# Up products of the feed-forward layers in seven blocks, down sums in three groups: one Trainium2 core

## The chip, the core and the metric

One core of a Trainium2 chip runs the whole program. The metric is device time in microseconds (us), the median of three runs. Each core has five engines with queues of their own: PE (TensorE, matrix products), DVE (VectorE), ACT (ScalarE), POOL (GpSimd) and SP (SyncE, which here only issues DMAs). They wait for one another through semaphores.

## What is computed

Two layers work on 512 tokens of width 1024, each layer a feed-forward (FFN), a mixer (even: gated linear and forgetting attention; odd: sparse attention) and a second FFN; a final norm follows. There are therefore four FFNs, called ffn0 to ffn3 here, with the even mixer between ffn0 and ffn1 and the odd one between ffn2 and ffn3. The change touches the FFNs, with d_ff = 2816:

```python
def swiglu(h, w_in, w_out):
    a, b = jnp.split(h @ w_in, 2, axis=-1)
    return (jax.nn.silu(a) * b) @ w_out

def reference(x, norm_g, ...):
    for layer in range(DEPTH):
        x = x + 0.5 * swiglu(rmsnorm(x, g[0]), ffn_w_in[layer, 0], ffn_w_out[layer, 0])
        x = x + mixer(rmsnorm(x, g[1]), ...)
        x = x + 0.5 * swiglu(rmsnorm(x, g[2]), ffn_w_in[layer, 1], ffn_w_out[layer, 1])
    return rmsnorm(x, final_norm_g)
```

All data are fp32. The kernel multiplies in the type float32r, with every operand split exactly into a high and a low part, so that one block product w x becomes three matmuls: high by high, high by low, low by high (`mm3`).

## The kernel before

The state X lies in SBUF as eight tiles of 128 channels by 512 tokens. **Norm.** The norm's gain is applied to X at once and its 1/rms later: `scaled` makes the parts XGH[i] (ACT, L139) and XGL[i] (DVE, L140) of X_i times the gain; `sumsq` adds X_i squared into one tile, the square on ACT (L152) and the add on POOL (L156). `rstd_cols` reduces that tile with four matmuls (L181) and takes the reciprocal root in short steps on ACT (L168, L169) and DVE (L184, L170 to L173); `rstd_tile` spreads the result over the partitions with four transposes (L195) into R.

**Way up.** `ffn` walks over 22 f tiles of 128 hidden channels. For each, `up_mm` loads 1024 KB of weights, splits them piece by piece (512 columns; high part on ACT L80, low part on DVE L84, pool `wsp` with six buffers) and runs 2 (gate and up) x 8 (channel tiles) x 3 matmuls of 512 tokens into two PSUM banks. `up_act` multiplies both by R on DVE (L231, L235), takes silu on ACT, multiplies (L236) and splits the result h in two (L209, L210). R is needed from `up_act(0)` on, and two or three `up_mm` stand ahead of it. **Way down.** After 12 of the 22 f tiles, `down(0, d)` sums f tiles 0 to 10 for each of eight output tiles d: 704 KB of weights, 11 x 3 matmuls of 512 tokens, and one DVE step (L247) that adds half of the sum to X_d. After the rest, `down(1, d)` does the same for f tiles 11 to 21, and `after(d)` starts the next layer's `scaled` and `sumsq` of X_d.

**Between layers.** The out projection of a mixer (`out_units`, 24 matmuls of 512 tokens for each d) ends with one DVE add (L323) and `after(d)`. Each weight is loaded into the two-buffer pool `wraw`, on SP's queue. **Order.** PE's instructions run in the order in which the code is written; a scheduler orders the other engines' queues, each of which then runs strictly in its order. **Start.** Nine matmuls of ones run ahead of the data; X and the first weights come in small pieces, interleaved, and `up_mm(0)` takes each channel tile as it comes.

In the addresses of the built program, the tiles of XGH and XGL start 32 bytes past a multiple of 64, and h, the mixers' outputs (the operand x of the out projection) and whi start on a multiple.

## Time and profile before

| | |
|---|---|
| median of 3 runs | 2019.51 us |
| the runs | 2015.47 to 2019.82 us |
| span of the profiled execution | 2014.5 us |
| PE busy | 1981.9 us (98%) |
| DVE, ACT, POOL busy | 1012.7, 765.4, 219.8 us |
| mean granted clock of PE | 0.993 |

The span is the time from the first to the last instruction of one profiled execution, whose own time is not given; the runs last 1.0 to 5.3 us longer than the span. The page says how long each engine was busy; the windows say it for one stretch; the timeline gives single instructions with their starts; a matmul's own duration overlaps the next one's, so its cost is the distance from start to start (called its pitch below).

### The profile page before, as it was taken

The page shows a single profiled execution, that of the slowest core. Times are in us where ns is not written, and L with a number is a line of the kernel's source. Part 1 is how long each engine was busy: PE and PEld are TensorE (multiplying, and loading weights), DVE is VectorE, ACT ScalarE, POOL GpSimd, SP SyncE. Part 2 cuts the span into 40 slices and gives each one's busy share as a digit, 9 for nine tenths or more (in the row PEclk, how much of TensorE's full clock was granted, in tenths as well). Part 3 has the DMA queues.
Part 4 walks back from the last instruction along what each step waited for, and adds up shares of the span by engine and source line. Part 5 has one row for each costly group of instructions (what it writes and reads, how often), then busy time and mean ns, then how long its engine had stood idle before and what let it go on. Part 6 is the DMA issues. An engine that isn't in the chain of part 4 may idle for free. (4 is left out here: it accounts for less than half of the span.)

```text
span 2014.5 us, 24213 instructions
## 1 busy us (share of the span) xinstructions
PE 1981.9 (98%) x9298; PEld 1602.2 (80%) x9298; DVE 1012.7 (50%) x1780; ACT 765.4 (38%) x1386; POOL 219.8 (11%) x230
## 2 busy tenths in 40 slices
PE   8999999999999999999999999999999999999997
PEld 6888888887878888888888888887777788888886
DVE  5543444457565444344444434444898654434443
ACT  4432333344454332233433323343537543322332
POOL 2000000100261000000100000001358410000001
PEclk9999999999899999999999999999999999999999
DMA  5223222213333222222222232223357122232222
GB/s 172 84 85 114 84 98 87 102 65 101 105 98 106 84 98 86 99 104 79 100 105 84 88 111 84 92 90 116 93 147 177 55 104 103 74 105 105 84 87 71
DMA packets 44212, 197.75 MB, mean 98 GB/s; under 512 B 6072, under 2 KB 7272, under 8 KB 29888
## 3 DMA queue, kind: packets, MB, share of 16 engines
q1 hardware_dynamic: 41440, 191.65, 28.8%
q10 hardware_dynamic: 2304, 4.20, 0.8%
q8 instruction: 73, 1.20, 0.2%
q0 software_dynamic: 352, 0.36, 0.1%
q14 instruction: 43, 0.35, 0.1%
HBM read 178.03 MB, written 2.15 MB: 89 GB/s over the span
## 5 line engine op out<-in xcount | busy, mean ns | idle before, releaser
L80 ACT ACTIVATE whi<-wraw 128x512 fp32r<-128x512 f32 (+2 forms) x667 | 411.6, 618 | 941.5 <-PE s L126 325.4
L84 DVE TENSOR_TENSOR wlo<-wraw,whi 128x512 fp32r<-128x512 f32 (+2 forms) x643 | 441.7, 688 | 496.1 <-ACT whi L80 462.7
L127 PE MATMUL s<-xgh,wlo 128*128 128x512 f32 x576 | 229.3, 398 | 1.9 <-DVE wlo L84 1.9
L126 PE MATMUL s<-xgl,whi 128*128 128x512 f32 x576 | 229.7, 399 | 1.3 <-DVE xgl L140 1.2
L125 PE MATMUL s<-xgh,whi 128*128 128x512 f32 x576 | 229.5, 398 | 1.1 <-ACT whi L80 1.1
L156 POOL TENSOR_TENSOR ss<-ss,sq 128x512 f32<-128x512 f32 x48 | 64.2, 1338 | 1495.6 <-ACT sq L152 1495.3
L125 PE MATMUL ps<-xgh,whi 128*128 128x512 f32 (+2 forms) x544 | 217.4, 400 | 1.6 <-DVE x L834 1.6
L127 PE MATMUL ps<-xgh,wlo 128*128 128x512 f32 (+2 forms) x544 | 215.6, 396 | 0.0
L126 PE MATMUL ps<-xgl,whi 128*128 128x512 f32 (+2 forms) x544 | 215.4, 396 | 0.0
L125 PE MATMUL pt<-xgh,whi 128*128 128x512 f32 x384 | 152.4, 397 | 0.0
L127 PE MATMUL pt<-xgh,wlo 128*128 128x512 f32 x384 | 152.3, 397 | 0.0
L126 PE MATMUL pt<-xgl,whi 128*128 128x512 f32 x384 | 152.2, 396 | 0.0
L127 PEld LDWEIGHTS s<-xgh,wlo 128*128 128x128 f32 x576 | 108.9, 189 | 29.6 <-DVE wlo L84 3.2
L126 PEld LDWEIGHTS s<-xgl,whi 128*128 128x128 f32 x576 | 108.9, 189 | 29.5 <-DVE xgl L140 3.5
L125 PEld LDWEIGHTS s<-xgh,whi 128*128 128x128 f32 x576 | 109.0, 189 | 28.2 <-ACT whi L80 1.7
L125 PEld LDWEIGHTS ps<-xgh,whi 128*128 128x128 f32 (+2 forms) x544 | 101.5, 187 | 28.0 <-issue 3.5
L127 PEld LDWEIGHTS ps<-xgh,wlo 128*128 128x128 f32 (+2 forms) x544 | 101.5, 187 | 25.8
L126 PEld LDWEIGHTS ps<-xgl,whi 128*128 128x128 f32 (+2 forms) x544 | 101.6, 187 | 24.3
L125 PE MATMUL s<-h,whi 128*128 128x512 f32 x264 | 102.7, 389 | 0.0
L126 PE MATMUL s<-h,whi 128*128 128x512 f32 x264 | 102.7, 389 | 0.0
L127 PE MATMUL s<-h,wlo 128*128 128x512 f32 x264 | 102.7, 389 | 0.0
L209 ACT ACTIVATE h<-tb 128x512 fp32r<-128x512 f32 x88 | 55.5, 632 | 115.9 <-DVE tb L236 115.7
(270 smaller groups left out, 3354.6 us busy)
## 6 DMA issues: line engine op xcount, KB each, us to landing
wraw<-in_ffn_in_dram SPq DMA_DIRECT2D x87, 1024.0 KB, 4.8
wraw<-in_ffn_out_dram SPq DMA_DIRECT2D x64, 704.0 KB, 4.1
x<-x SPq DMA_DIRECT2D x62, 128.0 KB, 2.4
wraw<-in_even_fox_dram SPq DMA_DIRECT2D x4, 1024.0 KB, 4.8
wraw<-in_even_out_dram SPq DMA_DIRECT2D x4, 1024.0 KB, 5.7
wraw<-in_odd_q_dram SPq DMA_DIRECT2D x8, 512.0 KB, 3.5
T<-rvd ACTq DMA_DIRECT2D x16, 256.0 KB, 4.3
wraw<-in_odd_out_dram SPq DMA_DIRECT2D x4, 1024.0 KB, 5.8
```

The source lines that it names most:

```text
L80: nc.scalar.activation(hi, x, AF.Copy)
L84: nc.vector.tensor_sub(lo, x, hi.bitcast(F32))
L125: mm(ps, w[0], x[0], start=first, stop=False)
L126: mm(ps, w[0], x[1], start=False, stop=False)
L127: mm(ps, w[1], x[0], start=False, stop=last)
L156: nc.gpsimd.tensor_tensor(self.ss, self.ss, sq, op=OP.add)
L209: self.nc.scalar.activation(o[0], x, AF.Copy)
```

## The change

Two f tiles make a pair p, 11 pairs for each FFN. The weights of a pair form blocks a11, a21, a12, a22 (of 128 partitions by 1024 columns: two f tiles times four channel tiles; the channel tiles split in even and odd ones, the columns in gate and up). The tokens are cut in two halves of 256 columns. A two by two block product that takes eight block products is written in the Strassen-Winograd form, with seven (p1 to p7) of sums and differences of blocks:

- `side` forms four combinations of weight blocks on DVE for each pair, and `make` splits seven blocks of 1024 columns (ACT L159, DVE L160), up to two products ahead. The pool `wsp` now holds three blocks of 1024 columns.
- `combined` takes the place of `scaled` ahead of an FFN: for each pair of channel tiles it forms seven token operands of 256 columns and splits them into TH and TL (L222, L223), with four differences on DVE (L229, L236 to L238). In the addresses of the built program, all operands of TH and TL start 32 bytes past a multiple of 64.
- `product` runs 2 x 4 x 3 = 24 matmuls of 256 columns for each product, 168 for each pair in place of 96 of 512. PE's order for a pair r is p1(r), p4(r-1), p5, p2, p6, p3, p7.
- The results are put together on ACT (copies c1, c5, c2) and DVE (L357, L363, L370, L374, L375); R multiplies the gate half (L365), and h is split for a pair at once (L378, L379).
- R is made between p6 and p3 of pair 0 of every FFN.
- The way down runs in three groups of pairs (4, 4 and 3) over all eight d. R is applied again to the up half in `down_end`, in two DVE steps (L396, L397).
- The weights of the mixers are split in pieces of up to 1024 columns; the nine matmuls of ones are gone; X and the blocks of pair 0 are loaded alternately; block a22 goes to a pool `wx` that lies where a mixer's memory lay.

```diff
+GROUPS = ((0, 4), (4, 8), (8, 11))
+HT = S // 2
+B11, T1, B21, B22, T2, T4, T3 = range(7)
...
+class Products:
+    ORDER = ("p1", "p5", "p2", "p6", "p3", "p7", "p4")
+    def __init__(self, b, src):
+        self.b, self.src, self.parts, self.blocks = b, src, {}, {}
+    def place(self, p, early):
+        b = self.b
+        w = self.blocks.setdefault(p, {})
+        if early:
+            raw = b.wraw.tile([128, 2048], F32, name="wraw")
+            w["a11"], w["a21"] = raw[:, :1024], raw[:, 1024:]
+            w["a22"] = b.wx.tile([128, 1024], F32, name="a22", bufs=2)
+        else:
+            w["a12"] = b.wx.tile([128, 1024], F32, name="a12", bufs=1)
+    def fetch(self, p, n):
+        c = ("a11", "a21", "a12", "a22").index(n) * 1024
+        self.b.nc.sync.dma_start(self.blocks[p][n], self.src[p, :, c:c + 1024])
+    def load(self, p, early):
+        if p < NP and ("a11" if early else "a12") not in self.blocks.get(p, ()):
+            self.place(p, early)
+            for n in ("a11", "a21", "a22") if early else ("a12",):
+                self.fetch(p, n)
+    def side(self, p, q):
+        w, v = self.blocks[p], self.b.nc.vector
+        if q == "p1":
+            return w["a11"]
+        if q == "p2":
+            return w["a12"]
+        if q == "p4":
+            return w["a22"]
+        if q == "p5":
+            w["s"] = self.b.wx.tile([128, 1024], F32, name="ws", bufs=1)
+            v.tensor_add(w["s"], w["a21"], w["a22"])
+            return w["s"]
+        if q == "p6":
+            v.tensor_sub(w["s"], w["s"], w["a11"])
+            return w["s"]
+        if q == "p3":
+            v.tensor_sub(w["a12"], w["a12"], w["s"])
+            return w["a12"]
+        v.tensor_sub(w["a21"], w["a11"], w["a21"])
+        return w["a21"]
+    def make(self, p, q):
+        if (p, q) in self.parts:
+            return
+        b = self.b
+        x = self.side(p, q)
+        o = b.wtile(1024)
+        b.nc.scalar.activation(o[0], x, AF.Copy)
+        b.nc.vector.tensor_sub(o[1], x, o[0].bitcast(F32))
+        self.parts[p, q] = o
...
-    def load_w(self, src, n, pool_lo=False, piece=512, cuts=()):
+    def load_w(self, src, n, pool_lo=False, piece=1024, cuts=()):
...
+    def combined(self, i, gcol):
+        nc, v = self.nc, self.nc.vector
+        j, x = i // 2, self.X[:, i].rearrange("p (h t) -> p h t", h=2)
+        def parts(n, m, src):
+            h, l = self.TH[j][:, n:n + m], self.TL[j][:, n:n + m]
+            nc.scalar.activation(h, src, AF.Copy)
+            v.tensor_sub(l, src, h.bitcast(F32))
+        if i % 2 == 0:
+            e = self.E = self.xp.tile([128, 3, HT], F32, name="te")
+            nc.scalar.activation(e[:, 0:3:2], x, AF.Copy, scale=gcol)
+            v.tensor_sub(e[:, 1], e[:, 2], e[:, 0])
+            parts(B11, 2, e[:, 0:2])
+        else:
+            e, o = self.E, self.xp.tile([128, 5, HT], F32, name="to")
+            nc.scalar.activation(o[:, 0:2], x, AF.Copy, scale=gcol)
+            parts(B21, 2, o[:, 0:2])
+            v.tensor_sub(o[:, 2], o[:, 1], e[:, 1])
+            v.tensor_sub(o[:, 3], o[:, 0], o[:, 2])
+            v.tensor_sub(o[:, 4], o[:, 1], e[:, 2])
+            parts(T2, 3, o[:, 2:5])
...
-        if first:
-            p = self.bank("o")
-            for _ in range(9):
-                nc.tensor.matmul(p[:, :128], self.ones, self.ones, start=True, stop=True)
...
+        def product(p, q, bank, t, fresh):
+            hi, lo = W.parts[p, q]
+            for f in range(2):
+                o = bank[:, f * HT:f * HT + HT]
+                for j in range(KT // 2):
+                    c = slice((f * 4 + j) * 128, (f * 4 + j) * 128 + 128)
+                    xh, xl = TH[j][:, t], TL[j][:, t]
+                    for i, (w, x) in enumerate(((hi, xh), (hi, xl), (lo, xh))):
+                        mm(o, w[:, c], x, start=fresh and f == j == i == 0, stop=j == 3 and i == 2, skip_group_check=True)
...
+            if q == "p1":
+                d = st[p] = {"a": self.bank("ps")}
+                product(p, q, d["a"], B11, True)
+                d["c1"] = copy("c1", d["a"], 1)
+                return
+            d = st[p]
+            if q == "p5":
+                d["b"] = self.bank("pt")
+                product(p, q, d["b"], T1, True)
+                d["c5"] = copy("c5", d["b"], 1)
+            elif q == "p2":
+                c = self.bank("s")
+                product(p, q, c, B21, True)
+                d["t"] = self.ft.tile([128, 2, 2, HT], F32, name="ta", bufs=2)
+                v.tensor_add(d["t"][:, :, 0], d["c1"], three(c))
+            elif q == "p6":
+                product(p, q, d["a"], T2, False)
+                d["c2"] = copy("c2", d["a"], 1)
+            elif q == "p3":
+                product(p, q, d["b"], B22, False)
+                v.tensor_add(d["t"][:, :, 1], d["c2"], three(d["b"]))
+                t = d["t"].rearrange("p f h t -> p f (h t)")
+                v.tensor_mul(t, t, R()[:, None, :].to_broadcast([128, 2, S]))
+                self.table = "silu"
+                nc.scalar.activation(t, t, AF.Silu)
+            elif q == "p7":
+                product(p, q, d["a"], T3, False)
+                v.tensor_add(d["c5"], d["c5"], three(d["a"]))
+            else:
+                product(p, q, d["a"], T4, False)
+                t = d["t"]
+                v.tensor_mul(t[:, :, 1], t[:, :, 1], d["c5"])
+                v.tensor_mul(t[:, :, 0], t[:, :, 0], three(d["a"]))
+                h = [self.hp.tile([128, 2, S], F32R, name=x) for x in ("hh", "hl")]
+                t = t.rearrange("p f h t -> p f (h t)")
+                nc.scalar.activation(h[0], t, AF.Copy)
+                v.tensor_sub(h[1], t, h[0].bitcast(F32))
+                H[p] = h
+                del st[p]
...
+        def down_end(d, bank, R):
+            t = self.ft.tile([128, S], F32, name="dn", bufs=1)
+            nc.vector.scalar_tensor_tensor(t, bank, 0.5, R, op0=OP.mult, op1=OP.mult)
+            nc.vector.tensor_add(self.X[:, d], self.X[:, d], t)
+        tags = ("s", "s", "s", "pt", "o")
+        Rt = []
+        R = lambda: Rt[0]
+        def round_(p, seq):
+            rc = None
+            for i, (r, q) in enumerate(seq):
+                for x in seq[i:i + 3]:
+                    W.make(*x)
+                if q == "p5" and (r + 1, "p1") in seq:
+                    W.load(r + 1, True)
+                if q == "p7":
+                    W.load(r + 1, False)
+                if (r, q) == (0, "p6"):
+                    rc = self.rstd_cols("o")
+                if (r, q) == (0, "p3"):
+                    Rt.append(self.rstd_tile(rc, "s"))
+                if (r, q) != (NP - 1, "p4"):
+                    run(r, q, R)
+        W.load(0, True)
+        W.load(0, False)
+        for g, (a, b) in enumerate(GROUPS):
+            last = b == NP
+            seq = []
+            for p in range(a + 1 if g else a, min(b + 1, NP)):
+                ps = [(p, q) for q in Products.ORDER[:6]]
+                if p:
+                    ps.insert(1, (p - 1, "p4"))
+                seq += ps
+            round_(a, seq + [(NP - 1, "p4")] * last)
+            banks = {}
+            def begin(d):
+                w = down_w(g, d)
+                w.split(0)
+                banks[d] = w, self.bank(tags[d % 5])
+            def sums(d, pairs):
+                down_mm(g, d, *banks[d], pairs)
+            def end(d):
+                down_end(d, banks.pop(d)[1], R())
+                if last:
+                    after(d)
+            begin(0)
+            begin(1)
+            if last:
+                self.next_in()
+                self.lnexp()
+                sums(0, range(a, b - 1))
+                run(NP - 1, "p4", R)
+                sums(1, range(a, b - 1))
+                for d in range(2):
+                    sums(d, [b - 1])
+                    end(d)
+                begin(2)
+            for d in range(2 if last else 0, KT):
+                if d + 1 < KT and d + 1 not in banks:
+                    begin(d + 1)
+                sums(d, range(a, b))
+                if d == KT - 2:
+                    W.load(b + 1, True)
+                end(d)
...
-        w = self.load_w(src, n, pool_lo, 512 // m * m)
+        w = self.load_w(src, n, pool_lo, 1024 // m * m)
...
         yield "last"
+        self.next_in()
...
-            self.wsp = pool("wsp", 6)
+            self.wsp = pool("wsp", 3)
...
+                for i, n in ((0, 0), (1, "a11"), (2, 0), (3, "a21"), (4, 0), (5, "a22"), (6, 0), (7, "a12")):
```

`self.next_in()` opens the pool of the next layer's operands; `copy` is an ACT copy out of PSUM, L336.

**The start, DVE.** Before, the queue took one operand of 512 tokens at a time between two pieces of weights (`xgl`, `wlo`):

```order
L140 SCALAR_TENSOR_TENSOR xgl0_91<-X_78,gn_79,xgh0_83 128x512
L84 TENSOR_TENSOR wlo_127<-wraw_107,whi_126 128x256
L84 TENSOR_TENSOR wlo_131<-wraw_107,whi_130 128x256
L140 SCALAR_TENSOR_TENSOR xgl1_92<-X_78,gn_79,xgh1_84 128x512
L140 SCALAR_TENSOR_TENSOR xgl2_93<-X_78,gn_79,xgh2_85 128x512
```

Now (te and to are the scratch tiles of `combined`; the rows are those on channel tiles 4 and 5 and the first on 6, the 17th to the 28th of the queue):

```order
L229 TENSOR_TENSOR te_159<-te_159 128x256
L223 TENSOR_TENSOR tl1_99<-to_147,th1_95 128x768
L150 TENSOR_TENSOR wraw_105<-wraw_105 128x1024
L223 TENSOR_TENSOR tl2_100<-te_159,th2_96 128x512
L236 TENSOR_TENSOR to_167<-to_167,te_159 128x256
L238 TENSOR_TENSOR to_167<-to_167,te_159 128x256
L237 TENSOR_TENSOR to_167<-to_167 128x256
L223 TENSOR_TENSOR tl2_100<-to_167,th2_96 128x512
L229 TENSOR_TENSOR te_179<-te_179 128x256
L160 TENSOR_TENSOR wlo_212<-ws_209,whi_211 128x1024
L223 TENSOR_TENSOR tl2_100<-to_167,th2_96 128x768
L223 TENSOR_TENSOR tl3_101<-te_179,th3_97 128x512
```

The operand tl3 that the last quarter of p1 reads now stands behind 26 DVE steps, among them two weight combinations and two splits.

**From the even mixer into ffn1, DVE.** Before, the last adds of the out projection (L323) and the operands of ffn1:

```order
L323 TENSOR_TENSOR X_78<-ps_5095,X_78 128x512
L84 TENSOR_TENSOR wlo_5202<-wraw_5182,whi_5201 128x512
L140 SCALAR_TENSOR_TENSOR xgl6_97<-X_78,gn_79,xgh6_89 128x512
L84 TENSOR_TENSOR wlo_5270<-wraw_5265,whi_5269 128x512
L323 TENSOR_TENSOR X_78<-ps_5138,X_78 128x512
L84 TENSOR_TENSOR wlo_5274<-wraw_5265,whi_5273 128x512
L140 SCALAR_TENSOR_TENSOR xgl7_98<-X_78,gn_79,xgh7_90 128x512
```

Now (L517 is the same add, ws_5955 the block for p5 of pair 0):

```order
L517 TENSOR_TENSOR X_78<-ps_5854,X_78 128x512
L229 TENSOR_TENSOR te_5888<-te_5888 128x256
L223 TENSOR_TENSOR tl3_5692<-te_5888,th3_5688 128x512
L517 TENSOR_TENSOR X_78<-ps_5896,X_78 128x512
L236 TENSOR_TENSOR to_5922<-to_5922,te_5888 128x256
L238 TENSOR_TENSOR to_5922<-to_5922,te_5888 128x256
L237 TENSOR_TENSOR to_5922<-to_5922 128x256
L223 TENSOR_TENSOR tl3_5692<-to_5922,th3_5688 128x512
L142 TENSOR_TENSOR ws_5955<-wraw_5944,a22_5945 128x1024
L223 TENSOR_TENSOR tl3_5692<-to_5922,th3_5688 128x768
L150 TENSOR_TENSOR wraw_5944<-wraw_5944 128x1024
L160 TENSOR_TENSOR wlo_5958<-ws_5955,whi_5957 128x1024
```

The split for p5 stands behind both halves of the work on the last two channel tiles, where the weights of the first f tiles were done ahead of it.

**R in ffn1, DVE.** Before:

```order
L184 TENSOR_SCALAR Ra_5255<-o_5250 128x4
L84 TENSOR_TENSOR wlo_5367<-wraw_5358,whi_5362 128x512
L170 TENSOR_TENSOR Ra_5255<-Ra_5255,rs_y_5258 128x4
L171 TENSOR_TENSOR Ra_5255<-Ra_5255,rs_y_5258 128x4
L172 TENSOR_SCALAR Ra_5255<-Ra_5255 128x4
L173 TENSOR_TENSOR Rc_5257<-rs_y_5258,Ra_5255 128x4
```

Now (wraw_5997 is block a11 of pair 1):

```order
L283 TENSOR_SCALAR Ra_6071<-o_6066 128x4
L150 TENSOR_TENSOR wraw_5997<-wraw_5997 128x1024
L160 TENSOR_TENSOR wlo_6108<-wraw_5997,whi_6107 128x1024
L269 TENSOR_TENSOR Ra_6071<-Ra_6071,rs_y_6074 128x4
L270 TENSOR_TENSOR Ra_6071<-Ra_6071,rs_y_6074 128x4
L271 TENSOR_SCALAR Ra_6071<-Ra_6071 128x4
L272 TENSOR_TENSOR Rc_6073<-rs_y_6074,Ra_6071 128x4
```

The four last steps of R now stand behind a split for p1 of the next pair, whose buffer is the one that p6 reads.

## Rows read from the trace of the kernel before

**Rows 1.** The page: busy time, share of the span and instructions of each engine.

```profile
PE 1981.9 (98%) x9298; PEld 1602.2 (80%) x9298; DVE 1012.7 (50%) x1780; ACT 765.4 (38%) x1386; POOL 219.8 (11%) x230
```

**Rows 2.** Windows: length, busy us (instructions) of each engine, granted clock, DMA.

```profile
20.00:22.00 2.00, 2.00 (x5) 1.62 (x6) 2.00 (x3) 0.64 (x2) 0.95 (x1) 0.50 0.00 0
200.00:330.00 130.00, 130.00 (x559) 104.93 (x558) 58.25 (x89) 43.46 (x68) 0.00 (x0) 1.00 0.26 90
800.00:900.00 100.00, 100.00 (x434) 81.30 (x434) 41.37 (x64) 29.31 (x47) 0.00 (x0) 1.00 0.29 99
940.00:970.00 30.00, 30.00 (x132) 24.56 (x131) 14.58 (x23) 12.42 (x20) 1.30 (x1) 1.00 0.27 91
```

**Rows 3.** Waits of PE: who waited for whom, total, times, longest.

```profile
PE pt L466 <- DVE pts L450: 3.9, 6, 1.0
PE s L426 <- DVE l L430: 3.5, 1, 3.5
```

**Rows 4.** PE's timeline, out projection into ffn1: start, duration, engine, line, operation, operands.

```profile
636.81 0.39 PE L125 MATMUL ps<-x,whi 128*128 128x512 f32 x1
...
642.02 0.39 PE L127 MATMUL ps<-x,wlo 128*128 128x512 f32 x1
642.25 0.40 PE L125 MATMUL s<-xgh,whi 128*128 128x512 f32 x1
...
645.06 0.40 PE L125 MATMUL s<-xgh,whi 128*128 128x512 f32 x1
```

**Rows 5.** PE's timeline in a mixer's products of 256 columns, moving whi.

```profile
404.01 0.28 PE L125 MATMUL ps<-whi,xgh 128*128 128x256 f32 x1
...
405.09 0.28 PE L125 MATMUL ps<-whi,xgh 128*128 128x256 f32 x1
```

**Rows 6.** Groups of instructions by form: count, busy us, mean ns of one, idle before.

```profile
L80 ACT ACTIVATE whi<-wraw 128x512 fp32r<-128x512 f32 x592 | 373.6, 632 | 851.3 <-PE s L126 288.5 <-PE ps L126 244.8 <-PE pt L126 190.9
L80 ACT ACTIVATE whi<-wraw 128x384 fp32r<-128x384 f32 x65 | 34.2, 526 | 86.2 <-PE s L126 36.9 <-PE ps L126 22.5 <-PE pt L126 20.0
L139 ACT ACTIVATE xgh<-X,gn 128x512 fp32r<-128x512 f32 x48 | 34.5, 720 | 17.0 <-DVE X L247 8.2 <-DVE X L323 6.2 <-DMA X<-in_x_dram 2.6
L450 DVE COPY pts<-pt 128x512 f32<-128x512 f32 x24 | 16.4, 681 | 5.8 <-PE pt L445 5.8
L450 DVE COPY pts<-pt 128x256 f32<-128x256 f32 x24 | 10.1, 419 | 0.0
L156 POOL TENSOR_TENSOR ss<-ss,sq 128x512 f32<-128x512 f32 x48 | 64.2, 1338 | 1495.6 <-ACT sq L152 1495.3
```

**Rows 7.** DVE's timeline in the out projection of the even mixer.

```profile
624.76 1.43 DVE L84 TENSOR_TENSOR wlo<-wraw,whi 128x512 fp32r<-128x512 f32 x1 [0.29 <-ACT whi L80]
626.13 0.69 DVE L323 TENSOR_TENSOR X<-ps,X 128x512 f32<-128x512 f32 x1
626.74 0.68 DVE L84 TENSOR_TENSOR wlo<-wraw,whi 128x512 fp32r<-128x512 f32 x1
```

**Rows 8.** POOL's timeline beside it.

```profile
624.35 1.29 POOL L156 TENSOR_TENSOR ss<-ss,sq 128x512 f32<-128x512 f32 x1 [3.78 <-ACT sq L152]
```

**Rows 9.** DVE's timeline at the start.

```profile
5.18 0.75 DVE L140 SCALAR_TENSOR_TENSOR xgl<-X,gn,xgh 128x512 fp32r<-128x512 f32 x1 [4.18 <-ACT xgh L139]
...
11.05 1.85 DVE L84 TENSOR_TENSOR wlo<-wraw,whi 128x256 fp32r<-128x256 f32 x2
...
15.20 2.92 DVE L84 TENSOR_TENSOR wlo<-wraw,whi 128x256 fp32r<-128x256 f32 x2
```

**Rows 10.** PE's timeline at the start; the second row is the 49th matmul of data.

```profile
5.50 0.79 PE L125 MATMUL s<-xgh,whi 128*128 128x512 f32 x1 [0.24 <-ACT whi L80]
...
25.46 0.40 PE L125 MATMUL pt<-xgh,whi 128*128 128x512 f32 x1
```

**Rows 11.** DVE's timeline, R in ffn1.

```profile
655.15 0.16 DVE L170 TENSOR_TENSOR Ra<-Ra,rs_y 128x4 f32<-128x4 f32 x1
...
655.74 0.16 DVE L173 TENSOR_TENSOR Rc<-rs_y,Ra 128x4 f32<-128x4 f32 x1
```

**Rows 12.** DMA issues: queue, count, size, median us from issue to landing.

```profile
wraw<-in_odd_q_dram SPq DMA_DIRECT2D x8, 512.0 KB, 3.5
wraw<-in_odd_uv_dram SPq DMA_DIRECT2D x2, 512.0 KB, 4.3
```

174 lines of the change are left out of this document (82 added, 92 removed).

## The prediction

> **What bounds the kernel now.** I read the busy shares first [rows 1]: PE works 1981.9 of 2014.5 us, DVE half of the time, ACT less. The windows say the same for each stretch of an FFN [rows 2]: between 200 and 330 us and between 800 and 900 us PE is busy without a break at full clock, DVE 41 to 45% and ACT 29 to 33%; and the change-over from ffn1 to ffn2 (940 to 970) has no gap either. The waits of PE are small, and the two largest lie in the attention [rows 3]. So the time of an FFN is its count of matmuls times their pitch, and whatever takes columns from PE counts in full as long as the other engines keep up. The reader should hold on to two things: the price of one matmul by its size, and how much DVE has left.
>
> **The price of a matmul.** In the out projection, where the moving operand starts on a multiple of 64 bytes, 23 matmuls of 512 columns take 642.02 - 636.81 = 5.21 us, 227 ns each. Right behind, with XGH and XGL, 12 take 2.81 us, 234 ns each [rows 4]. Matmuls of 256 columns with moving whi take 1.08 us for nine, 120 ns [rows 5]. The 227 and the 120 differ by the 107 ns of 256 columns, so each matmul has a fixed part of 13 ns whatever its length; the 7 ns on XGH and XGL I put down to their start address, since it is what sets them apart in the program. TH and TL start in the same way, and no row shows 256 columns with such a moving operand. Its bounds are 120 ns (no extra) and 127 ns (the 7 ns once for each matmul); between lies 120 x 234 / 227 = 124 ns (an extra for each column). Since the fixed part has proved to go by matmul, I take 127.
>
> By the Trainium skill (TensorE: Matmul & The Clock Gate, Back-to-back issue gap) an isolated matmul of N columns takes N / 2.4 + 2.5 ns on a warm engine, with no word on a start address. That would be 216 ns and 109 ns; the rows disagree with both, by 11 ns. By the page's figures a pair would gain 96 x 0.216 - 168 x 0.109 = 2.4 us, close to what the rows give without an extra.
>
> **What the seven products give.** A pair was 96 x 0.234 = 22.46 us and becomes 168 x 0.127 = 21.34 us: 1.12 us, over 44 pairs 50 us. At 124 ns it is 20.8 us and 72 us in all; at 120 ns 20.2 us and 101 us. The way down keeps its 528 matmuls of 512 columns in each FFN.
>
> **Does DVE keep up in steady state?** A pair costs DVE seven splits, four combinations, the product by R and the split of h, 13 steps of 1024 columns, and five of 512. From 256 to 512 columns a DVE step grows from 419 to 681 ns [rows 6], so 1024 columns take 0.68 + 2 x 0.26 = 1.2 us; queued steps start 0.08 us earlier than they end (0.61 apart, 0.69 long [rows 7]), so 1.13 us in a row. 13 x 1.13 + 5 x 0.61 = 17.7 us against 21.3 us of PE. ACT's step of 1024 columns takes 0.632 + 4 x 0.106 = 1.06 us [rows 6], and its 7 splits, 3 copies and the work on h stay under 13 us. PE remains the bound, with a DVE that goes from 45% to above 80%. The three buffers in `wsp` cover 3 us each, more than one split of 1.06 + 1.2 us. I put steady state at no stall; what is lost is lost at the seams, where the cover is thin.
>
> **The seams, one by one.**
>
> *R in each FFN.* PE needs R's column form for the transposes ahead of p3. In the DVE queue its last two to four steps now stand behind a split for the next pair's p1, and that split waits for p6's end, because p6 reads its buffer. After p6, PE therefore waits for ACT's high part (1.06), DVE's low part (1.2) and up to four steps at 0.2 us [rows 11]: 3.0 us, four times 12. Before, these steps followed one split of a free buffer, with the next `up_mm` running on PE. Bounds: 8 (2 us each, if ACT's part is half hidden) and 17 (with part of p3 at half clock after the wait, as in 20 to 22 us [rows 2]).
>
> *The start.* The last quarter of p1 needs tl3's first operand. Up to and with it stand 27 DVE steps: 13 of 256 columns (0.34), seven of 512 (0.61), three of 768 (0.87), four of 1024 (1.13), in all 15.8 us. The first can begin at 5.2 us, where the first XGL was made [rows 9]: 21.0 us. POOL's adds of squares run beside them; in rows 9 two short DVE steps took 1.85 and 2.92 us instead of 0.8, so 1.1 us more for each add that is met. With seven adds at 0.9 us the operand is there at 27 us. PE then has 15 matmuls of p1, p5 and p2 left, 63 x 0.127 = 8 us, and stands at 35 us with 9.1 us of work done: 26 us behind an ideal start. Before, 48 matmuls (11.2 us) were done at 25.46 us [rows 10]: 14.2 behind. The loss is 12; with a clock that is down after the waits [rows 2] I take 13. Bounds: 6 (POOL costs nothing) and 18. The nine matmuls of ones are part of this.
>
> By the Trainium skill (SBUF — State Buffer, SBUF: two separate sides) a DVE step with two SBUF inputs and a POOL step that reads SBUF exclude one another for the whole step. The trace agrees: a DVE split queued at 624.76 took 1.43 us and ended 0.55 us after POOL's add of 1.29 us had [rows 7, 8]. At the full 1.34 us for each of seven adds [rows 6] the start would lose 3 us more; that lies within the bound.
>
> *From a mixer into ffn1 and ffn3.* After the last matmul of the out projection the queue still holds, in series: for channel tile 6 the scale on ACT (0.72), a difference (0.42), both parts (0.63 and 0.68), 2.5 us; for tile 7 the add (0.69), scale (0.72), three differences (1.0) and a split (0.6), 3.0 us; the combination for p5 (1.13), a split of 768, a combination and p5's own split (0.87 + 1.13 + 1.13). That is 9.8 us, and 11.8 with two POOL adds. PE can do p1 and two more matmuls meanwhile, 26 x 0.127 = 3.3 us. Before, `up_mm(0)` covered 11 us of such work, and its weights had been split earlier. Stall 6.5 to 8.5; I take 8, twice 16, bounds 10 and 22. Block a22's transfer waits for the same last matmul, because its memory is the mixer's, and lands 3.5 to 4.3 us later [rows 12]; that is hidden behind tile 7, but is next in line.
>
> *From ffn1 to ffn2.* For two output tiles d DVE does four steps of `down_end` (2.4), the operands of an even and an odd channel tile (0.95 + 2.5) and two weight splits of 768 (1.7): 7.6 us, for eight 30.5. With five steps of 1024 for pair 0 (5.7) and seven POOL adds (6) it is 42 us. PE's cover is 8 x 18 x 0.227 = 32.7 and 1.1 of p1. I take 8; bounds 2 and 14.
>
> *The rest.* The last p4 of an FFN leaves a chain of 0.69 + 1.06 + 1.2 = 2.95 us under 12 matmuls (2.7 us), the short groups of 18 matmuls (4.1 us) leave little for `down_end` and `scaled`, and the mixers' first pieces are twice as long: 5 in all, bounds 0 and 10.
>
> Sum of losses: 12 + 13 + 16 + 8 + 5 = 54 us; the ends add up to 26 and 81, and since they are five separate things I expect 42 to 66.
>
> **The sum.** The profiled span of 2014.5 - 50 + 54 = 2018.5; the median of the runs lies 5.0 us above the span, so 2023.5, rounded to **2024 us**, with 2012 to 2036 for this case. Runs of this kernel can tell 0.2%, 4 us, from no change.
>
> **Rivals.**
>
> *TH and TL cost no extra (faster).* At 120 ns the gain is 101 and the time 2019.5 - 101 + 54 = 1972. For it speaks that no row shows the extra at this size; against it that it is steady on XGH and XGL. Break-even with before lies where the gain equals 54: 20.46 us saved down to 21.23 for a pair, 126.4 ns for a matmul. At 124 ns the time is 2019.5 - 72 + 54 = 2002.
>
> *The seams are half as dear (faster).* If the scheduler's queue lets DVE work ahead in the gaps that I filled, 27 instead of 54: 1997. Against it: each queue runs strictly in order.
>
> *DVE becomes the bound (slower).* It decides from the point where a pair on DVE exceeds 21.3 us, 3.6 us above the 17.7. Each product's split needs ACT's part first and a buffer that PE frees two products later, so waits add to the busy time. At 22 us a pair the stalls would add 44 x 0.7 = 31: 2055. Against it: 16% of slack, and buffers a product ahead.
>
> **How the numbers follow.** Forecast 0.55 (of it 0.1 under 2015.5, 0.13 within 4 us of before, the rest above); no extra 0.18; an extra by column 0.07; cheap seams 0.1; DVE bound 0.1. Faster: 0.1 + 0.18 + 0.06 + 0.09 = 0.43. Within 0.2%: 0.13 + 0.02 = 0.15. Slower: 0.32 + 0.1 = 0.42. Both signs hold much, so the range reaches from 1970, the case without an extra, to 2044, part of the way to a DVE bound.
>
> **What would show it.** The pitch of matmuls on TH and TL in the timeline (127, 124 or 120 ns) decides the first term; a pair in steady state should take 21.3 us with PE busy throughout and DVE 80 to 90%. Waits of PE for L272 should total 10 to 13 us, at the start p1 should wait for L223 until about 27 us, and p5 of ffn1 and ffn3 should wait for L159 and L160 by some 8 us. It is wrong if PE waits for DVE in every pair, or if the seams show half of these waits.

## The result and the profile after

The changed kernel takes **1968.1 us** (median, 1967.1 to 1969.3), against 2019.7 for the kernel before in the same series: ratio 0.974 with a 95% interval of 0.9725 to 0.9757. I had forecast 2024 us with a range from 1970 to 2044. The direction was wrong, and the time lies just below the range, at the rival in which TH and TL cost no extra (1972 us). Two errors of opposite sign made that: the gain from the matmuls was 127 us and not 50, and the seams lost 78 us and not 54.

The page of the kernel after; busy time, share of the span and instructions of each engine, beside [rows 1]:

```profile
span 1965.6 us, 30669 instructions
PE 1872.4 (95%) x12448; PEld 1682.0 (86%) x12448; DVE 1481.5 (75%) x1929; ACT 908.5 (46%) x1275; POOL 226.8 (12%) x218
```

PE has 110 us less to do, and 49 us of it show in the span: PE is idle for 93 us where it was idle for 33. DVE works half as much again. The windows (length, busy us and instructions of PE, weight loads, DVE, ACT, POOL, then PE's granted clock) show where; the first is a steady stretch of ffn0, the others are the seams into ffn1, ffn2 and ffn3, and answer to [rows 2]:

```profile
60.00:120.00 60.00, 60.00 (x517) 60.00 (x516) 56.85 (x56) 33.74 (x37) 0.00 (x0) 1.00 0.30 97
...
640.00:660.00 20.00, 12.31 (x80) 11.90 (x80) 17.33 (x17) 8.82 (x13) 0.99 (x1) 0.83 0.28 93
...
996.00:1016.00 20.00, 14.91 (x105) 14.42 (x105) 17.31 (x23) 9.18 (x15) 2.49 (x2) 0.82 0.23 80
1600.00:1620.00 20.00, 14.25 (x93) 13.71 (x91) 17.36 (x19) 8.76 (x11) 1.27 (x1) 0.74 0.26 94
```

In steady state PE has no gap although DVE is 95% busy there: PE remains the bound, by little. At the seams PE works 62 to 75% of the time, and at a lower clock. Who waited for whom (total, times, longest), for [rows 3]:

```profile
PE ps L332 <- ACT th L222: 15.2, 3, 7.5
PE ps L332 <- ACT whi L159: 12.8, 1, 12.8
PE s L294 <- DVE Rc L272: 11.4, 4, 3.0
PE pt L332 <- ACT whi L159: 9.0, 2, 4.5
PE ps L332 <- DVE tl L223: 7.8, 5, 3.5
```

These are the seams of the prediction: operands of the token side (L222, L223) at the start and into ffn2, R (L272) once in each FFN, p5's weights (L159) into ffn1 and ffn3. The price of a matmul is read from PE's timeline (start, duration):

```profile
249.84 0.28 PE L332 MATMUL ps<-th,wlo 128*128 128x256 f32 x1
...
251.94 0.28 PE L332 MATMUL ps<-th,wlo 128*128 128x256 f32 x1
```

18 matmuls in 2.10 us are 117 ns each, 10 less than I took and 3 less than the lower bound that [rows 5] gave.

### The profile page after: what moved, and what is told of

It is laid out like the page before. It is cut to its first block, busy times and chain, and to the rows that moved or that the text cites. A ratio compares the mean times of both kernels' runs of the same rounds, so it can differ in the third digit from the quotient of the medians.

```text
span 1965.6 us, 30669 instructions
## 1 busy us (share of the span) xinstructions
PE 1872.4 (95%) x12448; PEld 1682.0 (86%) x12448; DVE 1481.5 (75%) x1929; ACT 908.5 (46%) x1275; POOL 226.8 (12%) x218
## 4 chain that ended last, share of the span: by engine, by line
PE 82%; DVE 12%; ACT 2%; issue 2%; DMA 1%; SPq 0%; POOL 0%; DVEq 0%; ACTq 0%; POOLq 0%
PE ps L332 25%; PE pt L332 13%; PE s L332 6%; PE s L199 6%; PE s L200 6%; PE s L198 6%; PE ps L198 3%; PE ps L199 3%; PE ps L200 3%; DVE tl L223 2%; DVE acc L1108 1%; PE s L621 1%; PE pt L198 1%; PE pt L199 1%; PE pt L200 1%
## 5 line engine op out<-in xcount | busy, mean ns | idle before, releaser
L332 PE MATMUL ps<-th,whi 128*128 128x256 f32 x1408 | 395.5, 281 | 28.0 <-ACT th L222 15.2
L332 PE MATMUL ps<-tl,whi 128*128 128x256 f32 x1408 | 395.2, 281 | 7.8 <-DVE tl L223 7.8
L332 PE MATMUL ps<-th,wlo 128*128 128x256 f32 x1408 | 394.6, 280 | 1.0 <-DVE wlo L160 1.0
L332 PEld LDWEIGHTS ps<-th,whi 128*128 128x128 f32 x1408 | 266.4, 189 | 29.3 <-ACT th L222 15.9
L332 PEld LDWEIGHTS ps<-tl,whi 128*128 128x128 f32 x1408 | 266.4, 189 | 9.7 <-DVE tl L223 9.1
L332 PEld LDWEIGHTS ps<-th,wlo 128*128 128x128 f32 x1408 | 266.5, 189 | 1.3 <-DVE wlo L160 1.3
L159 ACT ACTIVATE whi<-a 128x1024 fp32r<-128x1024 f32 x132 | 140.2, 1062 | 154.1 <-PE pt L332 50.4
L332 PE MATMUL pt<-th,whi 128*128 128x256 f32 x704 | 200.9, 285 | 9.0 <-ACT whi L159 9.0
L199 PE MATMUL s<-hl,whi 128*128 128x512 f32 x528 | 206.0, 390 | 0.9 <-DVE hl L379 0.9
L198 PE MATMUL s<-hh,whi 128*128 128x512 f32 x528 | 205.6, 389 | 0.0
L200 PE MATMUL s<-hh,wlo 128*128 128x512 f32 x528 | 205.5, 389 | 0.0
L160 DVE TENSOR_TENSOR wlo<-a,whi 128x1024 fp32r<-128x1024 f32 x132 | 160.9, 1219 | 7.9 <-ACT whi L159 7.9
L159 ACT ACTIVATE whi<-wraw 128x1024 fp32r<-128x1024 f32 x88 | 93.4, 1061 | 145.6 <-PE ps L332 55.8
L396 DVE SCALAR_TENSOR_TENSOR dn<-s,R 128x512 f32<-128x512 f32 x72 | 49.7, 690 | 131.4 <-PE s L200 131.3
```

The lines of the kernel that those rows point to most:

```text
L159: b.nc.scalar.activation(o[0], x, AF.Copy)
L160: b.nc.vector.tensor_sub(o[1], x, o[0].bitcast(F32))
L198: mm(ps, w[0], x[0], start=first, stop=False)
L199: mm(ps, w[0], x[1], start=False, stop=False)
L200: mm(ps, w[1], x[0], start=False, stop=last)
L332: mm(o, w[:, c], x, start=fresh and f == j == i == 0, stop=j == 3 and i == 2, skip_group_check=True)
```

## The experiments

| run | what it changes | median us | ratio to before (95%) |
|---|---|---|---|
| after | | 1968.1 | 0.9741 (0.9725 to 0.9757) |
| e1_align | after, TH, TL, XGH, XGL on multiples of 64 | 1987.1 | 0.9854 (0.9826 to 0.9881) |
| e2_before_align | before, XGH, XGL on multiples of 64 | 2013.9 | 0.9973 (0.9963 to 0.9983) |
| e3_r_late | after, R behind p3 | 1952.5 | 0.9673 (0.9653 to 0.9692) |
| e4_p2_in_128 | after, p2 in 128 columns | 2064.2 | one run |
| e5_stagger | after, eight distances | 1979.3 | 0.9802 (0.9780 to 0.9823) |
| e6_before_same | before, XGH, XGL at distance 0 | 1986.6 | 0.9834 (0.9819 to 0.9849) |
| e7_squares_last | after, squares issued last | 1968.0 | 0.9737 (0.9716 to 0.9757) |
| e8_keep_busy | after, unused matmuls in the wait | 1961.1 | 0.9703 (0.9681 to 0.9725) |
| e9_no_adds | after, no POOL adds at the start | 1966.7 | 0.9737 (0.9716 to 0.9758) |
| e10_all_192 | after, TH, TL at distance 192 | 1961.7 | 0.9705 (0.9678 to 0.9732) |
| e11_steps_512 | after, pieces in steps of 512 | 1964.8 | 0.9727 (0.9698 to 0.9756) |
| e12_best | four edits together | 1948.4 | 0.9641 (0.9622 to 0.9661) |

The single runs of a kernel here spread over 2 to 10 us, so differences of less than about 5 us between two rows are not settled by the times alone; where I use them, the trace decides.

### Where the price of a matmul comes from

**e1_align** and **e2_before_align** move the start of the moving operands by 32 bytes, e1 with a small tile behind TL and one behind XGL:

```diff
                     self.TL = [self.xp.tile([128, 7, HT], F32R, name=f"tl{j}") for j in range(KT // 2)]
+                    self.xp.tile([128, 8], F32, name="pad")
...
                     self.XGL = [self.xp.tile([128, S], F32R, name=f"xgl{i}") for i in range(KT)]
+                    self.xp.tile([128, 8], F32, name="pad")
```

and e2 with one ahead of XGH and one behind XGL, where they are made first:

```diff
             self.gn = one("gn", [128, 7, KT])
+            one("pad", [128, 8])
...
             self.XGL = [one(f"xgl{i}", [128, S], F32R) for i in range(KT)]
+            one("pad2", [128, 8])
```

Expected of e1: 

> The kernel after, with one 32-byte tile more in the operands' pool, so that TH, TL and the mixers' XGH, XGL start on multiples of 64 bytes; nothing else moves. Theory A (the start address costs a moving operand something at any length, and something else hid it at 256 columns): the pitch on TH and TL falls from 117 ns to about 110, 7392 matmuls x 7 ns = 52 us, and the mixers' 512-column pitch on XGH and XGL from 234 to 227 ns (some 720 matmuls, 5 us): 1911 us. Theory B (the address costs 7 ns at 512 columns but at 256 another limit of 117 ns stands above it): TH and TL stay at 117 ns, the mixers go to 227: 1963 us. Theory C (the address has no part in it, XGH and XGL are slower for another reason): no pitch moves, 1968 us.

Expected of e2: 

> The kernel before, with two 32-byte tiles around XGH and XGL, so that these start on multiples of 64 bytes and all other tiles keep their start within 64. Theories A and B: the 4929 matmuls of 512 columns on them go from 234 to 227 ns, 34 us less: 1985 us. Theory C: 234 ns stays, 2019 us.

e1 is 19 us slower than after. On a multiple of 64, TH and TL cost more, not less; PE's timeline of e1:

```profile
219.78 0.28 PE L332 MATMUL ps<-th,whi 128*128 128x256 f32 x1
...
222.19 0.28 PE L332 MATMUL pt<-th,wlo 128*128 128x256 f32 x1
```

20 matmuls in 2.41 us are 120 ns, and the 7392 matmuls of the way up (44 x 168) at 3 ns more make 22 us, close to the measured loss of 19. In the mixers of the same run XGH and XGL went from 233 to 228 ns. e2 gained 6 us of the 34 expected; its timeline shows why:

```profile
249.88 0.40 PE L127 MATMUL s<-xgh,wlo 128*128 128x512 f32 x1
250.12 0.39 PE L125 MATMUL s<-xgh,whi 128*128 128x512 f32 x1
250.34 0.40 PE L126 MATMUL s<-xgl,whi 128*128 128x512 f32 x1
250.58 0.39 PE L127 MATMUL s<-xgh,wlo 128*128 128x512 f32 x1
250.81 0.40 PE L125 MATMUL s<-xgh,whi 128*128 128x512 f32 x1
...
251.28 0.40 PE L127 MATMUL s<-xgh,wlo 128*128 128x512 f32 x1
```

The pitch alternates, matmul by matmul, between some 229 and 238 ns, six in 1.40 us or 233 each: on average nearly what it was [rows 4]. None of theories A, B and C fits both runs. The start address alone is not it.

What differs between e2's XGH (233) and e1's (228) is how the tile lies to the *stationary* tiles. In the addresses of the built programs, modulo 512 bytes, the moving operand starts 0 bytes from the weights' parts for h in all kernels (227 ns) and for XGH in e1 (228), 416 bytes for XGH in before (234), 32 in after (233), 384 in e2 (233). **e6_before_same** tests that on the kernel before, by another order of the tiles in the first pool:

```diff
+            self.XGH = [one(f"xgh{i}", [128, S], F32R) for i in range(KT)]
+            self.XGL = [one(f"xgl{i}", [128, S], F32R) for i in range(KT)]
+            one("pad", [128, 48])
             self.gn = one("gn", [128, 7, KT])
...
             nc.sync.dma_start(self.gn, self.i["gains"])
-            self.XGH = [one(f"xgh{i}", [128, S], F32R) for i in range(KT)]
-            self.XGL = [one(f"xgl{i}", [128, S], F32R) for i in range(KT)]
```

**e5_stagger** tests it on 256 columns, with eight distances at once, by a small tile behind each tile of TH and TL (and e1's behind XGL):

```diff
-                    self.TH = [self.xp.tile([128, 7, HT], F32R, name=f"th{j}") for j in range(KT // 2)]
-                    self.TL = [self.xp.tile([128, 7, HT], F32R, name=f"tl{j}") for j in range(KT // 2)]
+                    t = []
+                    for j, pad in enumerate((32, 32, 32, 32, 64, 64, 128, 160)):
+                        t.append(self.xp.tile([128, 7, HT], F32R, name=("th", "tl")[j // 4] + str(j % 4)))
+                        self.xp.tile([128, pad // 4], F32, name=f"pad{j}")
+                    self.TH, self.TL = t[:4], t[4:]
```

Expected of e6: 

> The kernel before, with the tiles of the first pool in another order, so that XGH, XGL, h and the weights' parts all start at the same place modulo 512 bytes (distance 0). Theory F: the 4929 matmuls of 512 columns on XGH and XGL go from 234 to 227 ns, as those on h: 34 us less, 1985 us. Theory E: XGH and XGL on multiples of 64 as in the run that put them there at another distance, which moved 234 only to 233: 2013 us.

Expected of e5: 

> The kernel after, with gaps between the eight tiles of TH and TL, so that they start at eight different distances from the stationary tiles (modulo 512 bytes): th0 0, th1 32, th2 64, th3 96, tl0 128, tl1 192, tl2 256, tl3 384; the mixers' XGH and XGL at distance 0. Theory E (the start modulo 64 alone: 120 ns on a multiple, 117 ns off it): th1 and th3 at 117, the other six at 120, in all 44 x 168 x 2.3 = 17 us more than after, less 4 us in the mixers: 1981 us. Theory F (the distance from the stationary operand counts, 0 being the odd one): th0 near 120, all others near 117: 1966 us. Mixers in both: 228 ns for 234.

e6 is 34 us faster than before, as theory F said. Its timeline in the same place:

```profile
249.86 0.39 PE L127 MATMUL s<-xgh,wlo 128*128 128x512 f32 x1
...
251.22 0.39 PE L127 MATMUL s<-xgh,wlo 128*128 128x512 f32 x1
```

Six matmuls in 1.36 us, 227 ns, without the alternation. So at 512 columns the 7 ns belong to the distance between moving and stationary tile: shown for 0 against 32, 384 and 416 bytes. A period of 64 or 128 bytes is ruled out by the 384; one of 256 in place of 512 is not. At 256 columns e5 refutes both theories, although its 1979.3 us lie near the 1981 of theory E. By the mean distance from the start of a matmul to the start of the next in its up products, th0 (0) has 116.8 ns, th1 (32) 119.8, th2 (64) 117.3, th3 (96) 117.6, tl0 (128) 117.8, tl1 (192) 114.5, tl2 (256) 118.5 and tl3 (384) 119.6; all tiles at 0 gave 120 (e1), all at 32 gave 117 (after). Which tile such a distance belongs to is a matter of counting: from the start of the matmul before, tl1 has 123.3 ns and not 114.5. **e10_all_192** put all at the one that looked best:

```diff
                     self.TL = [self.xp.tile([128, 7, HT], F32R, name=f"tl{j}") for j in range(KT // 2)]
+                    self.xp.tile([128, 88], F32, name="pad")
```

Expected: 

> The kernel after with TH and TL at a distance of 192 bytes (modulo 512) from the stationary tiles; 32 in the kernel after gave 117 ns, 0 gave 120 ns. In the run with mixed distances the tile at 192 had 114.5 ns. If the distance of a tile from its own stationary operand sets its pitch, all 7392 matmuls go to 114.5: 16 us less, 1952 us. If what counted there was the change of distance from one matmul to the next, the pitch comes out at 117 or 120: 1968 to 1990 us.

```profile
100.06 0.28 PE L332 MATMUL ps<-th,whi 128*128 128x256 f32 x1
...
102.10 0.28 PE L332 MATMUL ps<-th,whi 128*128 128x256 f32 x1
...
219.79 0.28 PE L332 MATMUL s<-th,wlo 128*128 128x256 f32 x1
...
222.26 0.28 PE L332 MATMUL ps<-th,wlo 128*128 128x256 f32 x1
```

In ffn0's first group of pairs 18 matmuls in 2.04 us are 113 ns each; in its second group 21 in 2.47 us are 118, with the same tiles at the same addresses. All four FFNs show this: some 2900 matmuls at 113 ns, most of those ahead of the first way down, and some 4250 at 118. Against after, the stretch from p3 of pair 0 to the first way down is 2.3 to 2.4 us shorter in ffn0, ffn1 and ffn3 (not in ffn2), and the products of the second and third groups are together 1.1 us longer in every FFN (79.1 and 39.6 us for 78.4 and 39.2). So neither expectation came: at 256 columns the distance does not fix the pitch by itself. The level changed only where the row of matmuls was broken, by a wait of PE, R's matmuls, a way down or a change of clock; what chooses it stays open.

**e4_p2_in_128** asks what sets the level at 256.

```diff
-                        mm(o, w[:, c], x, start=fresh and f == j == i == 0, stop=j == 3 and i == 2, skip_group_check=True)
+                        for h in range(2 if q == "p2" else 1):
+                            u = slice(h * 128, h * 128 + 128) if q == "p2" else slice(0, HT)
+                            mm(o[:, u], w[:, c], x[:, u], start=fresh and f == j == i == h == 0, stop=j == 3 and i == 2, skip_group_check=True)
```

Expected: 

> The kernel after, with p2 of every pair as 48 matmuls of 128 columns in place of 24 of 256. If the load of the 128 stationary columns ahead of each matmul sets the 117 ns, 128 columns take 107 to 117 ns too: 44 x (48 x 0.112 - 2.8) = 113 us more. If a matmul costs its columns and a fixed 10 ns, 128 columns take 63 ns: 44 x (3.05 - 2.8) = 11 us more.

```profile
239.81 0.39 PE L334 MATMUL s<-tl,whi 128*128 128x128 f32 x2
...
242.71 0.39 PE L334 MATMUL s<-th,wlo 128*128 128x128 f32 x2
```

26 matmuls of 128 columns in 2.90 us are 112 ns each, hardly less than 117 with twice the columns, and the whole is 96 us slower (one run), near the 113 expected of a load and far from the 11 of a price by columns. So a row of such matmuls has a floor of some 112 ns that does not go by columns. Each matmul comes with the load of its 128 stationary columns, and this load is the likely cause, though no run took it away. By the Trainium skill (TensorE: Matmul & The Clock Gate, LDWEIGHTS (loading the stationary operand)) such a load takes P / 1.2 ns for P stationary columns, by estimate 107 ns for 128; the measured floor lies 5 ns above that. The load records of the traces last some 190 ns and overlap one another, so they do not give its cost. In the kernel before, two matmuls of 128 columns (L426, each with its own load) stand between matmuls of 512 columns, at full clock:

```profile
539.83 0.33 PE L426 MATMUL s<-x 128*128 128x128 f32 x2
540.00 0.44 PE L125 MATMUL ps<-xgh,whi 128*128 128x512 f32 x1
540.28 0.40 PE L126 MATMUL ps<-xgl,whi 128*128 128x512 f32 x1
```

The next matmul starts 0.17 us after the two, less than two floors; but the one behind it follows after 0.28 us in place of 0.23, so that the pair has cost 0.22 us in all, two floors, in part only later. That fits loads that queue up behind one another better than a price of the 128 columns themselves, which is argued and not shown. In a row of products, 256 columns stand right above the floor: a further halving of the tokens would gain nothing.

### Where the seams lose

**e3_r_late** makes R on PE where it is first used, behind p3, instead of ahead of it.

```diff
-        R = lambda: Rt[0]
+        rc = []
+        def R():
+            if not Rt:
+                Rt.append(self.rstd_tile(rc[0], "s"))
+            return Rt[0]
...
                 if (r, q) == (0, "p6"):
-                    rc = self.rstd_cols("o")
-                if (r, q) == (0, "p3"):
-                    Rt.append(self.rstd_tile(rc, "s"))
+                    rc.append(self.rstd_cols("o"))
```

Expected: 

> The kernel after, with R's four transposes behind p3 of pair 0 on PE instead of ahead of it. If the four waits for L272 (2.6 to 3.0 us each) are lost time, they go under p3: 11 us less and the half clock behind them with it, 1955 to 1957 us. Rival: the DVE queue is what is late at this seam, so PE waits the same time a product later: 1968 us.

It is 15.6 us faster than after. The same row in e3's waits:

```profile
PE s L294 <- DVE Rc L272: 3.2, 4, 1.1
```

11.4 us have become 3.2. The stretches from a seam to the first way down are 0.9, 4.5, 3.2 and 3.7 us shorter in ffn0 to ffn3, 12.3 in all for 8.2 us less of waiting; the other 3 us lie in the mixers, which this edit does not touch. So R was lost time as predicted, and a wait costs more than its length. **e8_keep_busy** shows the rest of that price.

```diff
+                if p == 0 and not first and n != 2:
+                    o = self.bank("o")
+                    for _ in range(36):
+                        mm(o[:, :HT], W.parts[0, "p1"][0][:, :128], TH[0][:, B11], start=True, stop=True)
```

Expected: 

> The kernel after, with 36 more matmuls (256 columns, results unused) behind p1 of pair 0 in ffn1 and ffn3, where PE waits 4.5 and 1.5 us for p5's weights. If the 43 to 46 matmuls at half clock behind each wait (about 5 us) come from PE having waited, they run at full clock: 2 x 5 = 10 us less, 1958 us. If the clock has another cause, or the added work (4.2 us) outlasts the wait, nothing or a loss: 1968 to 1972 us.

In the kernel after, PE's timeline behind the wait for p5's weights reads:

```profile
644.15 0.39 PE L332 MATMUL pt<-th,whi 128*128 128x256 f32 x1 [4.49 <-ACT whi L159]
...
646.20 0.58 PE L332 MATMUL pt<-th,wlo 128*128 128x256 f32 x1 [1.55 <-DVE wlo L160]
646.57 0.42 PE L332 MATMUL pt<-th,whi 128*128 128x256 f32 x1
...
648.50 0.41 PE L332 MATMUL pt<-th,whi 128*128 128x256 f32 x1
```

Nine matmuls in 1.93 us are 214 ns each, the pitch of 1.2 GHz, where 117 is that of 2.4. With the unused matmuls in the wait the windows that hold it (first and third line) show the full clock throughout, against 0.83 and 0.74 in after. The second line is the stretch behind, with R's wait, which this run keeps; its 0.91 is that of after:

```profile
640.00:660.00 20.00, 15.16 (x126) 14.56 (x126) 18.83 (x23) 9.88 (x15) 1.29 (x1) 1.00 0.32 104
660.00:680.00 20.00, 20.00 (x159) 20.00 (x158) 14.24 (x15) 11.24 (x12) 0.00 (x0) 0.91 0.17 58
1600.00:1620.00 20.00, 15.15 (x126) 14.55 (x125) 18.83 (x23) 10.06 (x15) 1.29 (x1) 1.00 0.33 107
```

The run is 7 us faster where 10 were expected; its trace shows 1.6 and 2.7 of them in the stretches into ffn1 and ffn3, and the rest is within the scatter. So the clock falls because PE waits, and keeping it up was worth 1.6 and 2.7 us. Not every wait does it: behind R's wait of 3.0 us the clock of after fell in ffn1 and ffn3, but in ffn2 it stayed at 1.00; the window of after:

```profile
1012.00:1032.00 20.00, 17.08 (x147) 17.08 (x148) 14.48 (x18) 11.78 (x15) 0.00 (x0) 1.00 0.21 75
```

**e7_squares_last** and **e9_no_adds** ask whether POOL's adds hold up DVE at the start. e7 makes all combinations first and then all squares:

```diff
             for i in range(KT):
-                start(i)
+                self.combined(i, self.gn[:, gi[st[0]], i:i + 1])
+            for i in range(KT):
+                self.sumsq(i)
```

e9 leaves the adds out:

```diff
-            else:
+            elif not self.no_adds:
...
+            self.no_adds = True
             for i in range(KT):
                 start(i)
+            self.no_adds = False
```

Expected of e7: 

> The kernel after, with the squares of the first norm and POOL's adds of them issued behind all token operands of ffn0 instead of between them. If POOL's adds hold up DVE at the start (ten DVE steps there took 0.3 to 1.1 us more than the same steps alone), tl3's first operand is there some 5 us earlier than 30.1 us and the whole ends 5 us earlier: 1963 us. Rival: the landing of X and ACT's row of steps set the pace, or the adds only meet the steps behind: 1968 us.

Expected of e9: 

> The kernel after without POOL's seven adds of squares at the first norm (the sum then holds the squares of one channel tile only); everything else is issued as before. The run with the squares issued last came out with the same order of steps, so it told nothing of this. If the adds hold up DVE at the start, the DVE steps beside them shrink to their own length, some 8 us over the first 24, and tl3's first operand comes at about 23 us instead of 30: up to 7 us less, 1961 us. Rival: ACT and DVE wait for one another for the scratch tiles te and to, and X lands too late: 1967 us.

e7's DVE queue has the same order and the same long steps: the scheduler puts the squares where they were, and the run told nothing. In e9 the steps are short. DVE's timeline at the start, of after:

```profile
14.45 1.50 DVE L236 TENSOR_TENSOR to<-to,te 128x256 f32<-128x256 f32 x1
15.87 1.48 DVE L238 TENSOR_TENSOR to<-to,te 128x256 f32<-128x256 f32 x1
...
29.45 0.68 DVE L223 TENSOR_TENSOR tl<-te,th 128x512 fp32r<-128x512 f32 x1
```

and of e9:

```profile
14.85 0.42 DVE L236 TENSOR_TENSOR to<-to,te 128x256 f32<-128x256 f32 x1
15.19 0.42 DVE L238 TENSOR_TENSOR to<-to,te 128x256 f32<-128x256 f32 x1
...
25.62 0.68 DVE L223 TENSOR_TENSOR tl<-te,th 128x512 fp32r<-128x512 f32 x1
```

tl3's first operand is there at 26.3 us instead of 30.1, and the first way down starts 2.8 us earlier. So the adds cost some 3 to 4 us of the start; the larger part is DVE's own row of steps, and the whole gained 1.4 us, which is within the scatter.

**e11_steps_512** looks at the mixers, which lost 5.3 and 4.1 us, by making the two parts of a weight piece in steps of 512 columns.

```diff
-        x = self.raw[:, c:c + m]
-        nc.scalar.activation(hi, x, AF.Copy)
+        for a in range(0, m, 512):
+            e = min(a + 512, m)
+            x, h, l = self.raw[:, c + a:c + e], hi[:, a:e], lo[:, a:e]
+            nc.scalar.activation(h, x, AF.Copy)
...
-            nc.vector.tensor_sub(lo, x, hi.bitcast(F32))
+                nc.vector.tensor_sub(l, x, h.bitcast(F32))
```

Expected: 

> The kernel after, with the pieces of 1024 columns of the mixers' and the way down's weights split in two steps of 512 columns each, into the same buffers. The mixers lost 5 and 4 us against the kernel before. If that comes from matmuls waiting for a step of double length, most of it comes back, 5 to 9 us: 1960 us. Rival: it comes from there being three buffers in place of six, or from the order of the queues: no gain, and 0.07 us more for each of some 230 added steps on DVE, which PE hides: 1968 us.

The even mixer came out 2.4 us shorter and the odd one 1.9 longer; the total moved by 3 us. In e3, which leaves the mixers as they are, the even one is 2.9 us shorter than in after, so the 2.4 is no sign of a gain. Not shown: what the mixers lost stays open between buffers, queues and the length of the steps.

**e12_best** takes four edits together: e3's, e8's with

```diff
-                    for _ in range(36):
+                    for _ in range(38):
```

e11's, and of e1's the tile behind XGL alone, for the mixers. Expected: 

> The kernel after with four edits together: R's transposes behind p3 (alone 15 us less), 38 unused matmuls behind p1 of pair 0 in ffn1 and ffn3 (with 36, 7 us less), the mixers' XGH and XGL at distance 0 from the stationary tiles modulo 512 (228 ns for 234 in the mixers, 4 us), and steps of 512 columns in the pieces of the mixers and of the way down (alone 3 us less, within its scatter). If the four losses are separate: 1968 - 15 - 7 - 4 - 3 = 1939 us. If one covers another (the keeping busy and the late R share the half clock behind the seam, or DVE has no room left): 1945 to 1955 us.

1948.4 us, 20 us below after and 73 below the kernel before in its own series, and 9 above the plain sum. The late R alone gave 15.6 of the 20. Its waits for R's column form (L274 here, L272 in after) are back at 5.8 us; that the other edits moved DVE's queue is likely and not shown.

```profile
PE s L296 <- DVE Rc L274: 5.8, 4, 2.7
```

## Why the prediction was wrong, point by point

**The price of a matmul: wrong, and it decided the sign.** The step that failed is "the 7 ns on XGH and XGL I put down to their start address", with its carrying over to 256 columns. The 234 ns were real, but they came from how XGH lay to the weights' tiles (e6: 227 ns and 34 us), not from its start (e2: 233); and at 256 columns no such extra stands on top (117 in after, 120 in e1). The bounds were wrong as well: I took the 120 ns of [rows 5] for the least possible, and called 13 ns a fixed part because 227 and 120 both had it. e4 shows another structure, a floor of 112 ns that does not go by columns. That 227 - 213 and 120 - 107 gave the same rest was two points on a line that I had no reason to draw. With the measured 78.4 us for four pairs, 19.6 a pair, and 96 x 0.2343 = 22.49 before, the gain is 44 x (22.49 - 19.60) = 127 us. Two slips in the arithmetic change nothing: 44 x 1.12 is 49 us and not 50, and the "20.46 us saved" of the break-even stands for the 22.46 us of a pair before.

**DVE in steady state: right.** No stall at 19.6 us a pair, though DVE is 95% busy there (56.85 of 60 us) where I said above 80%. With my 17.7 us this is 90%; the rest is that some steps of 1024 columns start 1.25 us apart and not 1.13, without a recorded wait.

**The seams: right places, too cheap.** From PE's timeline, each stretch less its matmuls at the steady pitch (0.2343 us for 512 columns on XGH before, 0.1167 us for 256 after):

| stretch | before | after | lost | predicted |
|---|---|---|---|---|
| start to ffn0's first way down (150.5, 130.1 us long) | 15.6 | 34.9 | 19 | 13 + 3 |
| even mixer's last matmul to ffn1's way down (136.3, 111.3) | 1.3 | 16.1 | 15 | 8 + 3 |
| ffn1's end to ffn2's way down (136.1, 111.6) | 1.2 | 16.4 | 15 | 8 + 3 |
| odd mixer's last matmul to ffn3's way down (136.3, 111.6) | 1.3 | 16.4 | 15 | 8 + 3 |
| the mixers (259.6 and 253.3, 264.9 and 257.4) | | | 9 | |
| the rest | | | 5 | 5 |

Together 78 us, 24 more than forecast. R was sized right: 11.4 us of waits for 12. The waits of PE in the other three seams, R's included, were also near the 11 forecast for each: 9.7, 12.2 and 9.4 us by its timeline, with 6.0 and 5.8 for p5 where I took 8. What was mis-sized is what stands behind a wait, the other 5, 3 and 6 us. I gave the half clock a place in the bounds and one microsecond in the terms, but a granted clock of 0.83 over 20 us is 6.8 us at the lower level, and e8 (1.6 and 2.7 us) and e3 (4.1 us beyond its waits) show the price. The waits into ffn2 and ffn3 in PE's timeline of after (in brackets; those into ffn1 for p5 stand at e8):

```profile
996.46 0.58 PE L332 MATMUL ps<-th,whi 128*128 128x256 f32 x1 [7.53 <-ACT th L222]
998.70 0.58 PE L332 MATMUL ps<-tl,whi 128*128 128x256 f32 x1 [1.66 <-DVE tl L223]
1014.92 0.65 PE L294 MATMUL s<-ident,Rc 128*128 128x128 f32 x4 [2.96 <-DVE Rc L272]
...
1605.96 0.58 PE L332 MATMUL pt<-th,whi 128*128 128x256 f32 x1 [4.50 <-ACT whi L159]
1608.01 0.58 PE L332 MATMUL pt<-th,wlo 128*128 128x256 f32 x1 [1.25 <-DVE wlo L160]
1623.11 0.65 PE L294 MATMUL s<-ident,Rc 128*128 128x128 f32 x4 [2.95 <-DVE Rc L272]
```

At the start DVE finished at 30 and not at 27 us. The two mixers, which I put under "the rest", lost 9 us by themselves, in one execution of each kernel; e3 shows that such figures move by 3 us. The order of the waits into ffn1 was as described: L142 stands directly behind tile 7's steps, without a gap, so a22's transfer was hidden. DVE's timeline of after:

```profile
639.09 0.42 DVE L236 TENSOR_TENSOR to<-to,te 128x256 f32<-128x256 f32 x1 [0.79 <-ACT to L234]
...
641.19 0.68 DVE L223 TENSOR_TENSOR tl<-to,th 128x512 fp32r<-128x512 f32 x1
641.79 1.21 DVE L142 TENSOR_TENSOR ws<-wraw,a 128x1024 f32<-128x1024 f32 x1
...
644.93 1.21 DVE L160 TENSOR_TENSOR wlo<-ws,whi 128x1024 fp32r<-128x1024 f32 x1
```

**The rivals.** "No extra" came true, at 1972 against 1968: by two errors that met, since its gain was 26 us too small and its losses 24 us too small, and that is luck. I gave it 0.18. The bound on DVE did not come.

## What to carry to other kernels

Before a change by a few per cent of a matmul's price is put on one cause, look for a second kernel or stage in which that cause is there and the price is not; here no row had that, and the bound of 120 ns should have been left open downwards. When a change takes work from the bound engine and loads the next one, add up the seams where there is no backlog, and count for each wait of PE the half clock that can follow it as well as its length; moving the wait behind the next product (e3) took 15.6 us off with a few lines. And a tile's place in memory is worth a run: e6 made the kernel before 34 us faster without touching its work. Against that kernel (1986.6 us) the change is worth 18 us and not 52, since some 30 of the 127 us gained on matmuls are the 7 ns on XGH and XGL, which a better place takes off as well.
